# Splitting queries and keys for two attention heads at once, with a DMA that moves the second head's rows

## The chip, the core and the metric

The kernel runs on one core of one Trainium2 chip. A core has five engines with a queue of instructions each, all working in order within their own queue: PE (TensorE, matrix products into PSUM), DVE (VectorE), ACT (ScalarE), POOL (GpSimd) and SP (SyncE, which here only issues DMAs). An instruction that waits on a semaphore holds up everything behind it in its own queue. The metric is the device time of one execution in microseconds (us), as a median over runs.

## The reference

One layer of a hybrid block on 512 tokens of 1024 features in float32: a gated linear attention (GLA) branch and a latent attention (MLA) branch are gated, added, projected, and followed by a feed-forward network. The change lies in the MLA branch, which computes this:

```python
q = (rmsnorm(cq, g_q) @ w_uq).reshape(B, S, H, 96)          # 8 heads, 64 plain + 32 rotary features
q = concatenate([q[..., :64], rope(q[..., 64:], positions)]) * 96 ** -0.5
kv = (rmsnorm(ckv, g_kv) @ w_ukv).reshape(B, S, H, 64 + 128)
k_nope, v = kv[..., :64], kv[..., 64:]
k = concatenate([k_nope, broadcast(rope(kr, positions))])    # the 32 rotary features are the same for all heads
p = softmax(q @ k.T)                                         # per head, 512 x 512
o = p @ v
```

## The kernel before

Every float32 operand of a product is split into a high part (rounded to the PE's fp32r format, by an ACT copy) and a low part (what is left, by a DVE subtraction). A product is then three PE passes, hi·hi, hi·lo and lo·hi (`mm3`, lines 88 to 90). `split` (lines 93, 94) makes the two parts; `split_scaled` (lines 97, 98) does so with a factor.

The MLA branch works head by head, and its inputs are made for a pair of heads at a time by the generator `up_units(pr)`, for the pairs 0 to 3:

- It loads the pair's weights (`wq…f`, `wk…f`, lines 1011 and 1017) and splits them on ACT and POOL.
- For each of the two heads a tile `q{pr}{i}` of 128 partitions x 2 x 512 (high and low part beside each other) is taken. Its partitions 0 to 63 are to hold the plain features, partitions 64 to 95 the rotary ones. The rotary rows were computed for all heads before, in the tiles `ro`; a DMA per half of 16 rows brings them (line 1034), two per head.
- `uq{pr}` is the product that gives the plain features of both heads in one PSUM tile: head 2·pr in partitions 0 to 63, head 2·pr+1 in partitions 64 to 127. Two calls of `split_scaled`, on 64 partitions each, write the parts to partitions 0 to 63 of the two `q` tiles.
- `uk{pr}` is the same for the keys. The parts go to partitions 0 to 63 of two of the four lasting tiles `kbuf0` to `kbuf3` (pairs 0 and 2 use 0 and 1, pairs 1 and 3 use 2 and 3). Partitions 64 to 95 of each `kbuf` hold the rotary key rows, written once by `rotary_k_split` (line 891) and never again.
- `uv{pr}` gives the values, in two tiles `v`.

The attention loop runs over n, four steps per head (a step is 128 queries), in a software pipeline. At step n it issues the scores of the step (`att_scores`: the product `s`, its row maximum `top` on DVE, line 1071, the exponential `e` on ACT, line 1076), the normalisation of an earlier pair of steps (lines 1081 to 1083), the transposition of step n-3 (`att_flip`: four transposes `tp` on PE, line 1091, then a split into `pT`), and every second step the product with the values (`av`, 24 passes for a head in two halves). The units of `up_units` for the next pair are spread between these steps. From line 1300 on other work is laid in too: the loads and sums of the output projection's weights (`bo10f`, `bo11f`, `bo20f`, `bo21f`, `w`), on SP and POOL.

The order on the queues in the attention loop is chosen by a scheduler at build time, under a few ordering hints (`goes_behind`); from the output projection on, PE, ACT and DVE keep the order of the program text.

Names used below: `s`, `tp`, `av`, `uq`, `uk`, `uv` with a head or pair number, so s of head 2 is the first score product that needs `q10` (pair 1, first head) and `kbuf2`.

Of the kernel before, what the change touches and what calls it, by code (L numbers as in the profile page):

```python
# [27 lines left out]
HALF = ROPE // 2  # L28
QK_SCALE = float((NOPE + ROPE) ** -0.5)
# [27 lines left out]
def tile_block(ctx: ExitStack, tc: tile.TileContext, t, out: bass.AP):  # L57
    nc = tc.nc
# [5 lines left out]
    def tl(shape, dt, tag, bufs, name):  # L64
        serial[0] += 1
        return sb.tile(shape, dt, tag=tag, bufs=bufs, name=f"{name}_{serial[0]}")
# [4 lines left out]
    def u4(name, dt=F32R, shape=(P, 2, S)):  # L71
        return tl(list(shape), dt, "u4", 26, name)
# [4 lines left out]
    def ps(tag, name):  # L77
        serial[0] += 1
        return pp.tile([P, S], F32, tag=tag, bufs=4, name=f"{name}_{serial[0]}")
# [4 lines left out]
    def raw(x):  # L84
        return x.bitcast(F32)

    def mm3(acc, lh, ll, rh, rl, start, stop, onto=False):
        nc.tensor.matmul(acc, lh, rh, start=start, stop=False, skip_group_check=onto)  # L88
        nc.tensor.matmul(acc, lh, rl, start=False, stop=False, skip_group_check=onto)  # L89
        nc.tensor.matmul(acc, ll, rh, start=False, stop=stop, skip_group_check=onto)  # L90

    def split(hi, lo, src, rest=nc.vector):
        nc.scalar.activation(hi, src, AF.Copy)  # L93
        rest.tensor_tensor(lo, src, raw(hi), op=ALU.subtract)  # L94

    def split_scaled(hi, lo, src, scale):
        nc.scalar.activation(hi, src, AF.Copy, scale=scale)
        nc.vector.scalar_tensor_tensor(lo, src, scale, raw(hi), op0=ALU.mult, op1=ALU.subtract)
# [8 lines left out]
    def traced():  # L107
        return len(nc.cur_bb.bb.instructions)
# [102 lines left out]
    def stage(nk, nw, name):  # L211
        wf = tl([P, nk, nw], F32, "wf", 3, f"{name}f")
        return wf

    def halves(nk, nw, name):
        wh = tl([P, nk, nw], F32R, "wh", 4, f"{name}h")
        wl = tl([P, nk, nw], F32R, "wl", 4, f"{name}l")
        return wh, wl
# [599 lines left out]
    def up_T(wh, wl, src, name):  # L818
        acc = ps("mm", name)
        n = len(src)  # L820
        for k in range(n):
            mm3(acc, wh[:, k, :], wl[:, k, :], src[k][:, 0, :], src[k][:, 1, :], k == 0, k == n - 1)
        return acc
# [38 lines left out]
    def rotary_q(accs):  # L862
        res = []
        for x in range(2):
            a, b = u2(f"roa{x}"), u2(f"rob{x}")
            ta, tb = (cos, sin) if x == 0 else (sin, cos)
            nc.vector.scalar_tensor_tensor(a, accs[0], QK_SCALE, ta, op0=ALU.mult, op1=ALU.mult)
            nc.vector.scalar_tensor_tensor(b, accs[1], QK_SCALE, tb, op0=ALU.mult, op1=ALU.mult)
            nc.vector.tensor_tensor(a, a, b, op=ALU.subtract if x == 0 else ALU.add)
            hl = u4(f"ro{x}")  # L870
            split(hl[:, 0, :], hl[:, 1, :], a)
            res.append(hl)
        return res
# [9 lines left out]
    def rotary_k_split():  # L883
        r = slice(64, 96)
        res = []
        for b in range(4):
            kb = u4(f"kbuf{b}")
            if b == 0:
                split(kb[r, 0, :], kb[r, 1, :], kr[r])
            else:  # L890
                nc.sync.dma_start(raw(kb[r]), raw(res[0][r]))
            res.append(kb)
        return res
# [113 lines left out]
    def up_units(pr):  # L1007

        wq = stage(3, P, f"wq{pr}")
        for k in range(3):  # L1010
            nc.sync.dma_start(
                wq[:, k, :].rearrange("p (h e) -> p h e", h=2), w_uq[:, k, 2 * pr : 2 * pr + 2, 0:NOPE]
            )
        wqh, wql = halves(3, P, f"wq{pr}")
        split(wqh, wql, wq, nc.gpsimd)
        wk = stage(2, 384, f"wk{pr}")
        nc.sync.dma_start(
            wk.rearrange("p k (h e) -> p k h e", h=2), w_ukv[:, :, 2 * pr : 2 * pr + 2, :]
        )
        wh, wl = halves(2, 384, f"wk{pr}")  # L1020
        src = wk.rearrange("p k (h e) -> p k h e", h=2)
        for k in range(2):
            for c, e in ((slice(0, 128), slice(0, NOPE)), (slice(128, 384), slice(NOPE, 192))):
                split(wh[:, k, c].rearrange("p (h e) -> p h e", h=2),
                      wl[:, k, c].rearrange("p (h e) -> p h e", h=2), src[:, k, :, e], nc.gpsimd)
        if pr == 0:
            yield
        qs = []
        for i in range(2):
            q = u4(f"q{pr}{i}")  # L1030
            h = (2 * pr + i) * HALF
            for x in range(2):
                at = NOPE + x * HALF
                nc.sync.dma_start(raw(q[at : at + HALF]), raw(ro[x][h : h + HALF]))
            qs.append(q)
        yield
        accq = up_T(wqh, wql, cq, f"uq{pr}")
        for i in range(2):
            split_scaled(qs[i][0:64, 0, :], qs[i][0:64, 1, :], accq[i * 64 : i * 64 + 64, :], QK_SCALE)
        yield  # L1040
        acck = up_T(wh[:, :, 0:128], wl[:, :, 0:128], ckv, f"uk{pr}")
        for i in range(2):
            kb = kbuf[2 * (pr % 2) + i]
            split(kb[0:64, 0, :], kb[0:64, 1, :], acck[i * 64 : i * 64 + 64, :])
        yield
        vs = []
        for j in range(2):
            acc = ps("mm", f"uv{pr}{j}")
            for i in range(2):
                tok = slice((2 * j + i) * P, (2 * j + i + 1) * P)  # L1050
                for k in range(2):
                    mm3(acc[:, i * 256 : i * 256 + 256], ckv[k][:, 0, tok], ckv[k][:, 1, tok],
                        wh[:, k, 128:384], wl[:, k, 128:384], k == 0, k == 1)
            hl = u4(f"v{pr}{j}", F32R, (P, 2, 2, 256))
            flat = [hl[:, x].rearrange("p a b -> p (a b)") for x in range(2)]
            split_scaled(*flat, acc, 0.5)
            vs.append(hl)
            yield
        for i in range(2):
            heads[2 * pr + i] = (qs[i], kbuf[2 * (pr % 2) + i], vs, slice(i * MV, (i + 1) * MV))  # L1060
# [99 lines left out]
    for n, (a, m) in enumerate(steps[:-4]):  # L1160
# [4 lines left out]
        if steps[n + 1] in fillers:  # L1165
            at = traced()
# [106 lines left out]
    h = GH - 1  # L1273
# [10 lines left out]
    kbuf = rotary_k_split()  # L1284
# [5 lines left out]
    ckv = ckv_.normed()  # L1290
    accs = [up_T(*w, cq, f"ro{x}") for x, w in enumerate(wr)]
    units = up_units(0)
    next(units)
    ro = rotary_q(accs)
# [9 lines left out]
    at = traced()  # L1304
# [5 lines left out]
    in_program_order(pooled, (mybir.EngineType.Pool,))  # L1310
    LAG_B, LAG_C = 3, 6
    units = up_units(1)
    at = traced()
    next(units)
# [3 lines left out]
    for n in range(4 * MH + LAG_C - 1):  # L1318
# [12 lines left out]
        if 2 <= n % 8 < 7:  # L1331
            at = traced()
# [5 lines left out]
        if n in (6, 14):  # L1338
            units = up_units(n // 8 + 2)
            at = traced()  # L1340
            next(units)
            if n == 6:
                goes_behind((at, traced()), span["fourth"], SPLITTERS[:1])
# [28 lines left out]
        if n == 17:  # L1372
            at = traced()
# [246 lines left out]
    at = traced()  # L1620
# [9 lines left out]
    at = traced()  # L1630
# [7 lines left out]
    at = traced()  # L1638
# [12 lines left out]
    at = traced()  # L1651
# [81 lines left out]
```

## Time and profile before

| what | value |
|---|---|
| median of 3 runs | 757.4 us (757.4 to 757.45) |
| the profiled execution, its own time | 757.7 us |
| its span, first to last instruction | 755.7 us |
| instructions | 10257 |
| HBM read, written | 83.25 MB, 2.10 MB |
| first score product to the last of the attention loop's steps | about 298 to 376 us of the span |

Times within an execution are counted from the start of the span. A line of a profile names the engine, the source line and operation, the tile written and the tiles read, the shapes, how often it occurs, and after a bar the busy time and the mean duration of one in ns. PEld is the PE's loading of weights, SPq the issuing of a DMA by SP. "To landing" is the time from a DMA's issue until its completion arrives.

### The profile page before, as it was taken

To read this page: it belongs to the slowest core of one execution; us is meant where nothing else is said; L and a number is where in the kernel's file an instruction comes from. 1 tells how busy PE (TensorE), PEld (TensorE's weight loads), DVE (VectorE), ACT (ScalarE), POOL (GpSimd) and SP (SyncE) were. 2 spreads that over 40 slices of the span, in tenths; PEclk is the share of its full clock that TensorE was granted. 3 is DMA by queue.
4 is the path that set the end of the run, shared out by engine and by line. 5 is a ranking of instruction groups with operands and counts; after the bars stand their busy time and mean duration, and the time that the engine had idled before them with its cause. 6 is when DMAs were issued, how large, how long until landed. Compare 5 with 4: busy or idle time off the path is not lost.

```text
span 755.7 us, 10257 instructions
## 1 busy us (share of the span) xinstructions
PE 746.8 (99%) x3720; PEld 632.8 (84%) x3720; DVE 586.5 (78%) x850; ACT 461.6 (61%) x780; POOL 165.3 (22%) x238
## 2 busy tenths in 40 slices
PE   9999999999999999999999999999999999999996
PEld 7888888888889888898888988888888888888885
DVE  7777887989787597898897787856696578748795
ACT  8456565686476575988865766345544555345644
POOL 0722110262662632136850100000000000000014
PEclk9999999999999999999999999999999999999999
DMA  9849582611321334228897421461126410650003
GB/s 315 256 125 230 177 174 82 113 29 29 83 57 31 47 86 114 73 84 198 264 201 227 129 57 56 140 194 57 56 65 204 122 57 4 206 153 0 29 1 111
DMA packets 94306, 87.59 MB, mean 116 GB/s; under 512 B 15696, under 2 KB 66896, under 8 KB 94256
## 3 DMA queue, kind: packets, MB, share of 16 engines
q1 hardware_dynamic: 87760, 74.33, 32.8%
q0 software_dynamic: 6208, 12.32, 9.3%
q8 instruction: 29, 0.48, 0.3%
q10 hardware_dynamic: 288, 0.28, 0.1%
q14 instruction: 21, 0.17, 0.1%
HBM read 83.25 MB, written 2.10 MB: 113 GB/s over the span
## 4 chain that ended last, share of the span: by engine, by line
PE 93%; DVE 3%; ACT 2%; DMA 1%; issue 1%; POOL 0%; POOLq 0%; ACTq 0%; SPq 0%
PE f L90 8%; PE f L88 8%; PE f L89 8%; PE gx L88 4%; PE gx L90 4%; PE gx L89 4%; PE first L330 3%; PE gz L90 2%; PE gz L88 2%; PE gz L89 2%; PE zb L88 1%; PE tp L1091 1%; PE zb L90 1%; PE zb L89 1%; PE wox L88 1%; PE wox L90 1%
## 5 line engine op out<-in xcount | busy, mean ns | idle before, releaser
L1672 POOL DMA_DIRECT2D gfin<-in_g_final x1 | 0.6, 628 | 284.1 <-PE f L90 284.1
L961 DVE TENSOR_TENSOR w<-w,w 128x1024 f32<-128x1024 f32 x32 | 38.7, 1221 | 0.3
L1071 DVE TENSOR_REDUCE top<-s 128x1 f32<-128x512 f32 x32 | 21.8, 682 | 2.9 <-PE s L90 2.6
L1076 ACT ACTIVATE e<-s,top 128x512 f32<-128x512 f32 x32 | 22.0, 689 | 2.7 <-DVE top L1071 2.4
L94 DVE TENSOR_TENSOR pT<-tp,pT 128x512 fp32r<-128x512 f32 x32 | 21.6, 682 | 2.4 <-ACT pT L93 2.2
L1399 DVE TENSOR_TENSOR h<-h,gx 128x512 f32<-128x512 f32 x32 | 21.5, 682 | 1.9 <-PE gx L90 1.8
L93 ACT ACTIVATE pT<-tp 128x512 fp32r<-128x512 f32 x32 | 18.9, 597 | 3.2 <-PE tp L1091 3.0
L1091 PE MATMUL tp<-ident,e 128*128 128x128 f32 x128 | 19.3, 274 | 0.4 <-ACT e L1082 0.2
L88 PE MATMUL av<-pT,v 128*128 128x256 f32 x64 | 18.9, 296 | 0.0
L93 ACT ACTIVATE ghb<-y 128x512 fp32r<-128x512 f32 x16 | 10.1, 633 | 14.0 <-DVE y L907 14.0
L1465 ACT ACTIVATE fa<-f 128x512 f32<-128x512 f32 x32 | 18.5, 578 | 0.0
L1091 PEld LDWEIGHTS tp<-ident,e 128*128 128x128 f32 x128 | 15.1, 140 | 3.9 <-ACT e L1082 0.8
L89 PE MATMUL av<-pT,v 128*128 128x256 f32 x64 | 18.2, 285 | 0.0
L90 PE MATMUL av<-pT,v 128*128 128x256 f32 x64 | 18.2, 285 | 0.0
L547 ACT ACTIVATE bds<-bd 128x512 f32<-128x512 f32 x4 | 2.4, 598 | 20.9 <-PE bd L543 20.9
L93 ACT ACTIVATE b_00h<-w 128x1024 fp32r<-128x1024 f32 x7 | 7.4, 1061 | 12.6 <-PE gz L90 6.0
L93 ACT ACTIVATE b_20h<-w 128x1024 fp32r<-128x1024 f32 x7 | 7.4, 1062 | 12.1 <-PE gz L90 6.0
L93 ACT ACTIVATE b_10h<-w 128x1024 fp32r<-128x1024 f32 x7 | 7.4, 1061 | 12.1 <-PE gz L90 6.0
L88 PE MATMUL s<-kbuf,q 96*128 96x512 f32 x32 | 14.2, 444 | 0.1
L1474 ACT ACTIVATE px<-fa 128x256 f32<-128x256 f32 x32 | 13.4, 418 | 1.0
L957 POOL DMA_DIRECT2D w<-in_w_out x10 | 12.3, 1401 | 6.5 <-DVE bo60l L94 5.3
L636 POOL DMA_DIRECT2D gvw<-in_w_in x4 | 4.8, 1226 | 38.7 <-DVE gvw L641 34.0
(1731 smaller groups left out, 2947.8 us busy)
## 6 DMA issues: line engine op xcount, KB each, us to landing
w<-in_w_ff SPq DMA_DIRECT2D x64, 256.0 KB, 3.4
w<-in_w_out POOLq DMA_DIRECT2D x10, 512.0 KB, 8.8
grw<-in_w_in SPq DMA_DIRECT2D x8, 512.0 KB, 9.3
zaw<-in_w_in SPq DMA_DIRECT2D x8, 512.0 KB, 7.9
gvw<-in_w_in SPq DMA_DIRECT2D x8, 512.0 KB, 4.5
w<-in_w_out SPq DMA_DIRECT2D x16, 256.0 KB, 5.9
x<-in_xt SPq DMA_DIRECT2D x8, 256.0 KB, 5.2
vw<-in_w_first SPq DMA_DIRECT2D x8, 256.0 KB, 5.4
```

Source lines behind the costliest of these rows:

```text
L88: nc.tensor.matmul(acc, lh, rh, start=start, stop=False, skip_group_check=onto)
L89: nc.tensor.matmul(acc, lh, rl, start=False, stop=False, skip_group_check=onto)
L90: nc.tensor.matmul(acc, ll, rh, start=False, stop=stop, skip_group_check=onto)
L93: nc.scalar.activation(hi, src, AF.Copy)
L94: rest.tensor_tensor(lo, src, raw(hi), op=ALU.subtract)
L330: nc.tensor.matmul(f_accs[i], a[:, i * P : (i + 1) * P], b, start=k == 0 and x == 0, stop=k == KD - 1 and x == 2)
L961: nc.vector.tensor_tensor(wq[dst][g], wq[x][g], wq[y][g], op=op)
L1071: nc.vector.tensor_reduce(top, acc, axis=AX.X, op=ALU.max, negate=True)
L1076: nc.scalar.activation(e, acc, AF.Exp, bias=top, accum_out=tot[:, qt % 2 : qt % 2 + 1])
L1091: nc.tensor.transpose(tp[:, k * P : (k + 1) * P], e[:, k * P : (k + 1) * P], ident)
L1399: nc.vector.tensor_tensor(hc, hc, acc, op=op)
L1465: nc.scalar.activation(a, acc, AF.Relu)
```

## The change

Pair 0 stays as it was (`apart`). For pairs 1 to 3:

- The split of `uq` is one `split_scaled` over all 128 partitions into the first head's tile. A DMA moves partitions 64 to 127 of it to partitions 0 to 63 of the second head's tile. After it two DMAs bring the first head's rotary rows to its partitions 64 to 95, which the split and the move had used. The second head's rotary rows still come before the product, as they did.
- The split of `uk` is one `split` over all 128 partitions into the first of the pair's two `kbuf` tiles. It overwrites the rotary key rows there. A DMA moves partitions 64 to 127 to the second `kbuf`, and another brings the rotary rows (partitions 64 to 95) back from the second `kbuf` to the first.

```diff
@@ -1025,23 +1025,38 @@
-        qs = []
-        for i in range(2):
-            q = u4(f"q{pr}{i}")
+        def rotary_rows(i):
             h = (2 * pr + i) * HALF
             for x in range(2):
                 at = NOPE + x * HALF
-                nc.sync.dma_start(raw(q[at : at + HALF]), raw(ro[x][h : h + HALF]))
-            qs.append(q)
+                nc.sync.dma_start(raw(qs[i][at : at + HALF]), raw(ro[x][h : h + HALF]))
+        apart = pr == 0
+        qs = [u4(f"q{pr}{i}") for i in range(2)]
+        for i in range(2):
+            if apart or i == 1:
+                rotary_rows(i)
         yield
         accq = up_T(wqh, wql, cq, f"uq{pr}")
-        for i in range(2):
-            split_scaled(qs[i][0:64, 0, :], qs[i][0:64, 1, :], accq[i * 64 : i * 64 + 64, :], QK_SCALE)
+        if apart:
+            for i in range(2):
+                split_scaled(qs[i][0:64, 0, :], qs[i][0:64, 1, :], accq[i * 64 : i * 64 + 64, :], QK_SCALE)
+        else:
+            split_scaled(qs[0][:, 0, :], qs[0][:, 1, :], accq, QK_SCALE)
+            nc.sync.dma_start(raw(qs[1][0:64]), raw(qs[0][64:128]))
+            rotary_rows(0)
         yield
         acck = up_T(wh[:, :, 0:128], wl[:, :, 0:128], ckv, f"uk{pr}")
-        for i in range(2):
-            kb = kbuf[2 * (pr % 2) + i]
-            split(kb[0:64, 0, :], kb[0:64, 1, :], acck[i * 64 : i * 64 + 64, :])
+        kbs = kbuf[2 * (pr % 2) : 2 * (pr % 2) + 2]
+        if apart:
+            for i, kb in enumerate(kbs):
+                split(kb[0:64, 0, :], kb[0:64, 1, :], acck[i * 64 : i * 64 + 64, :])
+        else:
+            split(kbs[0][:, 0, :], kbs[0][:, 1, :], acck)
+            nc.sync.dma_start(raw(kbs[1][0:64]), raw(kbs[0][64:128]))
+            nc.sync.dma_start(raw(kbs[0][64:96]), raw(kbs[1][64:96]))
         yield
```

## The prediction

> **What bounds the kernel now.** First the page's busy shares and its chain of work that ended last.
>
> ```profile
> PE 746.8 (99%) x3720; PEld 632.8 (84%) x3720; DVE 586.5 (78%) x850; ACT 461.6 (61%) x780; POOL 165.3 (22%) x238
> PE 93%; DVE 3%; ACT 2%; DMA 1%; issue 1%; POOL 0%; POOLq 0%; ACTq 0%; SPq 0%
> ```
>
> PE is busy 99% of the span and is 93% of the chain. The averages hide the stages, so next the stretches: busy time of each engine in the attention loop and around it, then one crowded part of the loop, then PE's waits in the loop.
>
> ```profile
> core 0: us, PE busy (x) PEld busy (x) DVE busy (x) ACT busy (x) POOL busy (x), PEclk, DMA share, GB/s
> 284.00:298.00 14.00, 13.74 (x72) 11.72 (x71) 9.59 (x16) 6.99 (x14) 3.09 (x6) 1.00 0.43 87
> 298.00:382.00 84.00, 83.49 (x556) 74.64 (x555) 74.25 (x130) 73.71 (x159) 42.32 (x50) 1.00 0.56 152
> 382.00:420.00 38.00, 38.00 (x182) 31.80 (x182) 33.25 (x53) 23.36 (x44) 8.66 (x12) 1.00 0.88 228
> ...
> 310.00:320.00 10.00, 9.85 (x64) 8.64 (x63) 9.27 (x17) 10.00 (x24) 3.27 (x5) 1.00 0.45 110
> ...
> PE tp L1091 <- ACT e L1082: 0.2, 1, 0.2
> ```
>
> In the 84.00 us of the loop PE is busy 83.49: it stands still 0.51 us in all, and one named wait is 0.2 of it. DVE (74.25) and ACT (73.71) are nearly as full, and ACT has no idle time between 310 and 320, yet PE loses only 0.15 there. So PE's own work sets this stage's length, with the others close behind. The clock is at 1.00 throughout.
>
> **What is removed.** Per pair 1 to 3 the change takes away one ACT copy and one DVE operation for the queries, and as much for the keys. These groups give durations; the `v` rows are the same operations on 128 partitions.
>
> ```profile
> L97 ACT ACTIVATE v<-uv 128x512 fp32r<-128x512 f32 x6 | 3.6, 598 | 1.4 <-PE uv L90 1.2
> L97 ACT ACTIVATE q<-uq 64x512 fp32r<-64x512 f32 x6 | 3.6, 593 | 0.7 <-PE uq L90 0.4 <-DVE q L98 0.3
> L93 ACT ACTIVATE kbuf<-uk 64x512 fp32r<-64x512 f32 x6 | 3.6, 592 | 0.6 <-PE uk L90 0.5
> ...
> L94 DVE TENSOR_TENSOR kbuf<-uk,kbuf 64x512 fp32r<-64x512 f32 x6 | 4.1, 687 | 1.1 <-ACT kbuf L93 1.0
> L98 DVE SCALAR_TENSOR_TENSOR q<-uq,q 64x512 fp32r<-64x512 f32 x6 | 4.1, 687 | 0.9 <-ACT q L97 0.7
> L98 DVE SCALAR_TENSOR_TENSOR v<-uv,v 128x512 fp32r<-128x512 f32 x6 | 4.1, 683 | 0.0
> ```
>
> Doubling the partitions is free: 598 against 593 ns on ACT, 683 against 687 on DVE. So six instructions of 0.59 us leave ACT (3.6 us) and six of 0.69 leave DVE (4.1 us). Neither engine ends the stage. PE's instructions stay the same in number and shape, so what can come back is PE's idle time: at most 0.51 us, at least nothing. I take half, 0.3 us, because the named wait is on ACT and relief there should remove it, while other gaps follow from the scheduler's order and may reappear.
>
> **What is added.** Nine DMAs: for each pair a 256 KB move of `q` and one of `kbuf` (64 partitions of 4 KB), and a 128 KB return of the rotary key rows. Two rotary-row DMAs of the first head move from before `uq` to behind the move. None is on PE's path until a score product of the pair's first head waits for it. That product needs both ends of two chains: split, move, then rotary rows; split, move, then return. The second DMA of a chain overwrites rows that the first one reads, so SP must wait for the first landing. Before, the first head needed only its split. The second head, four steps later, needs only the moves. The landings of the trace, and what SP's issue takes:
>
> ```profile
> q<-ro SPq DMA_DIRECT2D x16, 64.0 KB, 2.3
> w<-in_w_out SPq DMA_DIRECT2D x16, 256.0 KB, 5.9
> bo11f<-in_w_out SPq DMA_DIRECT2D x2, 256.0 KB, 3.0
> ...
> kbuf<-kbuf SPq DMA_DIRECT2D x3, 128.0 KB, 3.6
> ...
> 290.65 2.42 SPq L1034 DMA_DIRECT2D q<-ro  x4
> ...
> 302.00:310.00 8.00, 8.00 (x56) 7.21 (x54) 5.36 (x10) 7.23 (x14) 0.00 (x0) 1.00 0.00 1
> 346.00:360.00 14.00, 13.77 (x100) 12.36 (x99) 12.73 (x22) 11.33 (x25) 8.73 (x10) 1.00 0.83 192
> ```
>
> No row shows a 256 KB move within SBUF. Below lies the 256 KB load at 3.0; above, the straight line through the two SBUF copies, 2.3 at 64 KB and 3.6 at 128 KB, gives 6.2. I take 3.6: the 128 KB copies shared the engines with weight loads, while the moves of pair 1 start in a stretch where the DMA engines do nothing (share 0.00). The return is the same operation as the copy at 3.6; bounds are 2.3 and 5.9 (the loads in the crowded stretch). An issue is 2.42/4 = 0.6 us.
>
> Pair 1, where the first head comes soonest. In time order: the splits, then the place of head 2 on PE.
>
> ```profile
> 304.51 0.67 DVE L98 SCALAR_TENSOR_TENSOR q<-uq,q 64x512 fp32r<-64x512 f32 x1
> 306.16 0.69 DVE L98 SCALAR_TENSOR_TENSOR q<-uq,q 64x512 fp32r<-64x512 f32 x1
> 306.89 0.69 DVE L94 TENSOR_TENSOR kbuf<-uk,kbuf 64x512 fp32r<-64x512 f32 x1
> ...
> 311.38 0.27 PE L1091 MATMUL tp<-ident,e 128*128 128x128 f32 x1
> ...
> 315.37 0.40 PE L88 MATMUL s<-kbuf,q 96*128 96x512 f32 x1
> ...
> 318.30 1.12 ACT L93 ACTIVATE bo11h<-bo11f 128x1024 fp32r<-128x1024 f32 x1
> ```
>
> `q10` is whole at 304.51 + 0.67 = 305.2. The key split moves up into the slot of the second query split, 306.16 to 306.9. Query chain: 305.2 + 3.6 = 308.8, two issues to 310.0; the second starts at 309.4 and lands 2.3 later, at 311.7. Key chain: 306.9 + 3.6 = 310.5, + 3.6 = 314.1. The build keeps head 2 at nearly the same place on PE: between the last transposes of head 0 (311.38) and s of head 2 it puts s of head 1, twenty `av` passes and one group of transposes, 0.35 + 0.7 + 20 x 0.12 + 0.35 = 3.8 us, so about 315.2. The margin is 315.2 - 314.1 = 1.1 us, by the lower bounds 306.9 + 3.0 + 2.3 = 312.2 it is 3.0, by the upper ones of an idle DMA (6.2 + 3.6) the data are 1.5 late.
>
> Behind these waits on SP stand the next pair's second-head rotary rows and `bo11f`: return issued at 310.5, three issues, `bo11f` at 312.3, landed 315.3, three us before ACT's split at 318.30. That is hidden by `bo11h`'s place late in ACT's queue.
>
> Pairs 2 and 3, by the first key split and the first score product of heads 4 and 6:
>
> ```profile
> 325.44 0.67 DVE L94 TENSOR_TENSOR kbuf<-uk,kbuf 64x512 fp32r<-64x512 f32 x1
> 346.36 0.68 DVE L94 TENSOR_TENSOR kbuf<-uk,kbuf 64x512 fp32r<-64x512 f32 x1
> ...
> 336.16 0.39 PE L88 MATMUL s<-kbuf,q 96*128 96x512 f32 x1
> 358.57 0.48 PE L88 MATMUL s<-kbuf,q 96*128 96x512 f32 x1
> ```
>
> In the build the scheduler has set the pair 2 split behind more DVE work, which I count as 0.7 later: 326.8 + 7.2 = 334.0 against 336.2, margin 2.2. Pair 3: 347.0 + 7.2 = 354.2 against 358.6, margin 4.4; with 5.9 for both, 358.8, just late, because DMA is 0.83 busy from 346 on. The loads `w` queued behind the pair 3 return start near 351; before, eight of them started at 352.
>
> ```profile
> 352.08 4.97 SPq L951 DMA_DIRECT2D w<-in_w_out  x8
> ```
>
> So nothing downstream moves either. The sum: 757.7 for the profiled execution - 0.3 + 0 for the DMAs = 757.4. That execution lies 0.3 above the median of 757.4, so the forecast for the median is 757.1, rounded to 757.2 for the chance of a small new gap.
>
> **The rivals.** *A, slower: the key rows of the pair's first head land late.* It decides once move plus return take longer than 315.2 - 306.9 = 8.3 us at head 2, or 336.2 - 326.8 = 9.4 at head 4. With 6.2 + 3.6 = 9.8 PE stands 1.5 us at head 2 and 0.4 at head 4: 757.2 + 1.9 = 759.1. With 6.2 + 5.9 it stands 3.8, 2.7 and 0.5: 764.2. For it speaks that no row shows such a move, and that PE has nothing else it may run, being in order; against it the 3.0 of `bo11f` and the empty DMA at 302 to 310. I price it at 760. The Trainium skill ("TensorE: Matmul & The Clock Gate", Part 1: the HAM clock gate) says that about 3.4 us of idling halves PE's clock until some 3.4 us of work have passed. By that page the worst case would cost about 1.7 us more (an estimate from its figures); no stretch quoted here idles long enough to show it.
>
> *B, slower: the new order of the queues makes waits of its own.* ACT and DVE are reordered through the loop. A PE wait in the loop is 0.2 us in the row above; one more for each of some twelve reordered steps would be 2.4 us: 759.6. Against it: ACT and DVE have less to do than before.
>
> *C, faster: ACT and DVE bound the loop, and PE's busy time covers waits.* For it: ACT's 10.00 of 10.00. Then ACT's 3.6 us come off: 753.8. Against it: start to start, score passes run at the pace of passes where nothing else is crowded.
>
> ```profile
> 295.29 0.39 PE L88 MATMUL zb<-xT,zb7h 128*128 128x512 f32 x1
> 295.52 0.39 PE L89 MATMUL zb<-xT,zb7h 128*128 128x512 f32 x1
> ...
> 298.01 0.40 PE L88 MATMUL s<-kbuf,q 96*128 96x512 f32 x1
> 298.25 0.40 PE L89 MATMUL s<-kbuf,q 96*128 96x512 f32 x1
> ```
>
> Both steps are 0.23 to 0.24 us. The Trainium skill ("Perfetto Trace Analysis", Identifying the Most-Contended Engine) holds that matmul busy share is a poor measure of how near PE is to its limit, since matmuls are pipelined, and that the weight-load share should be used. By that share the loop has 74.64 of 84 us, so the page leaves room for C; the pace just shown speaks against it.
>
> That the change does nothing it says is excluded: the build has six ACT and six DVE instructions fewer and nine DMAs more.
>
> **How the numbers follow.** About 0.2%, 1.5 us, is what a measurement of this kernel can tell from no change. Forecast (757.2, own range 756.4 to 758.6): 0.66. A: 0.20, of which a quarter stays under 1.5 us. B: 0.08, half of it under. C: 0.06, all over. So faster 0.06, slower 0.15 + 0.04 = 0.19, raised to 0.22 because A's prices rest on an operation that no row shows; same 0.72. The range reaches to A's priced case with some room above and stops short of C: 756.3 to 760.3.
>
> **What would show it.** Right: `q` and `kbuf` groups with three 128x512 entries each; the moves landing in 3 to 4 us; s of heads 2, 4 and 6 without idle time before them; PE idle in the loop at or below 0.5 us; a span within 1 us of 755.7. Wrong: idle time of PE ahead of s of head 2, released by a DMA (A); PE waits on ACT or DVE scattered through the loop (B); a loop shorter by more than 1 us at full PE (C).

## The result and the profile after

The changed kernel takes 762.2 us (median of 6 runs, 761.6 to 762.9); the kernel before takes 757.5 us on the same chip (median of 6, 757.4 to 758.3). The ratio is 1.0061, 95% interval 1.0050 to 1.0072. The change makes the kernel slower by 4.7 us, where no measurable change was forecast (757.2, range 756.3 to 760.3).

Shares of the span first (engine, busy us, share, instructions), then the groups of ACT for the two splits inside the attention loop. Both are of the changed kernel.

```profile
PE 748.7 (99%) x3720; PEld 634.6 (83%) x3720; DVE 582.5 (77%) x844; ACT 457.6 (60%) x774; POOL 164.2 (22%) x238
```

```profile
L97 ACT ACTIVATE q<-uq 128x512 fp32r<-128x512 f32 x3 | 1.8, 595 | 0.0
L93 ACT ACTIVATE kbuf<-uk 128x512 fp32r<-128x512 f32 x3 | 1.8, 591 | 1.4 <-PE uk L90 1.4
```

The change did what it says: six instructions fewer on ACT (780 to 774) and on DVE (850 to 844), and one on 128 partitions costs what one on 64 did (595 and 591 against 593 and 592 ns). ACT and DVE are 4.0 us less busy each. And PE, whose instructions are the same, is 1.9 us *more* busy (746.8 to 748.7). A busy time that grows with the same work is a sign to look at the clock. First the waits of PE, then stretches of the loop: length, busy time of PE, PEld, DVE, ACT and POOL, granted clock, DMA share, GB/s.

```profile
PE s L88 <- DMA kbuf<-kbuf: 3.0, 1, 3.0
```

```profile
298.00:382.00 84.00, 81.00 (x534) 72.65 (x533) 65.79 (x118) 65.82 (x146) 39.37 (x48) 0.98 0.68 175
358.00:360.00 2.00, 0.00 (x0) 0.00 (x0) 1.14 (x3) 0.45 (x1) 2.00 (x4) 1.00 1.02 228
...
362.00:363.00 1.00, 1.00 (x4) 0.70 (x4) 0.62 (x2) 0.86 (x2) 0.00 (x0) 0.57 0.94 315
363.00:364.00 1.00, 1.00 (x6) 0.94 (x5) 1.00 (x2) 0.41 (x2) 0.00 (x0) 0.50 0.85 283
364.00:365.00 1.00, 1.00 (x7) 1.00 (x7) 0.06 (x1) 0.84 (x3) 0.00 (x0) 0.50 1.11 256
365.00:366.00 1.00, 1.00 (x8) 1.00 (x8) 0.00 (x0) 0.42 (x1) 0.00 (x0) 0.73 1.05 242
```

There is one stop of PE, 3.0 us, and it is the whole idle time of the loop (84.00 - 81.00). Behind it the granted clock falls to 0.57, 0.50, 0.50 and 0.73 in four successive microseconds: 0.43 + 0.50 + 0.50 + 0.27 = 1.7 us of PE time lost while PE counts as busy. Stop and clock make 4.7 us of PE time. That the medians differ by 4.7 us too is in part chance, since the change also gains about 1 us; the account stands further down. The chain of waits shows where the stop stands (start, us, what).

```profile
352.17 0.34 SPq L1032
...
352.56 0.60 SPq L1032
...
353.27 7.32 DMA kbuf<-kbuf
...
360.73 0.47 PE s L88
```

The first score product of head 6 waits for the return of the rotary key rows of pair 3, issued at 353.27 and landed at 360.59. Next SP's queue, then the DMAs issued in that stretch with KB and us from issue to landing.

```profile
342.05 0.42 SPq L967 DMA_DIRECT2D bo21f<-in_w_out  x1
342.57 0.38 SPq L224 DMA_DIRECT2D f00f<-in_w_ff  x1
344.48 0.50 SPq L1048 DMA_DIRECT2D q<-q  x1
346.99 0.50 SPq L1058 DMA_DIRECT2D kbuf<-kbuf  x1
351.96 1.19 SPq L1032 DMA_DIRECT2D q<-ro  x2
353.27 0.53 SPq L1059 DMA_DIRECT2D kbuf<-kbuf  x1
```

```profile
w<-in_w_out POOLq DMA_DIRECT2D x2, 512.0 KB, 8.3
f00f<-in_w_ff SPq DMA_DIRECT2D x1, 512.0 KB, 8.0
...
q<-q SPq DMA_DIRECT2D x1, 256.0 KB, 7.4
kbuf<-kbuf SPq DMA_DIRECT2D x1, 256.0 KB, 5.7
q<-ro SPq DMA_DIRECT2D x2, 64.0 KB, 7.0
kbuf<-kbuf SPq DMA_DIRECT2D x1, 128.0 KB, 7.3
```

The query move needs 7.4 us and lands at 351.9. SP waits for it before it may issue the rotary rows, and the return stands behind these two issues although the key move landed at 346.99 + 5.7 = 352.7, which costs it 0.6 us. Then the return itself takes 7.3 us, beside two accumulating loads of `w` from POOL's queue. Pair 1, in an empty stretch, is the contrast:

```profile
q<-q SPq DMA_DIRECT2D x1, 256.0 KB, 2.9
kbuf<-kbuf SPq DMA_DIRECT2D x1, 256.0 KB, 2.8
...
kbuf<-kbuf SPq DMA_DIRECT2D x1, 128.0 KB, 2.3
```

The same three kinds of copy take 2.3 to 2.9 us there, and heads 2 and 4 start without a wait. So the trace leaves a theory and rivals: are pair 3's copies slow because of what stands ahead of them in SP's queue (`f00f`), because of the bytes of `f00f` and of POOL's loads whatever their queue, or because three copies in a chain are too many in any case?

### The profile page after: what moved, and what is told of

It is laid out like the page before. It is cut to its first block, busy times and chain, and to the rows that moved or that the text cites. A ratio compares the mean times of both kernels' runs of the same rounds, so it can differ in the third digit from the quotient of the medians.

```text
span 760.1 us, 10265 instructions
## 1 busy us (share of the span) xinstructions
PE 748.7 (99%) x3720; PEld 634.6 (83%) x3720; DVE 582.5 (77%) x844; ACT 457.6 (60%) x774; POOL 164.2 (22%) x238
## 4 chain that ended last, share of the span: by engine, by line
PE 95%; DVE 2%; DMA 1%; ACT 1%; issue 0%; POOL 0%; SPq 0%; POOLq 0%
PE f L88 8%; PE f L90 8%; PE f L89 8%; PE gx L88 4%; PE gx L90 4%; PE gx L89 4%; PE first L330 3%; PE gz L88 2%; PE gz L90 2%; PE gz L89 2%; PE tp L1106 2%; PE zb L88 1%; PE zb L90 1%; PE zb L89 1%; PE s L88 1%; DMA kbuf<-kbuf 1%
## 5 line engine op out<-in xcount | busy, mean ns | idle before, releaser
L1097 ACT ACTIVATE e<-e,tot 128x512 f32<-128x512 f32 x16 | 11.6, 725 | 4.5 <-DVE tot L1096 4.5
```

## The experiments

Each kernel was run beside the kernel before on one chip. The medians of before in these comparisons are 757.8 to 757.9 us.

**Pair 3 left apart.**

```diff
-        apart = pr == 0
+        apart = pr in (0, 3)
```

> The last pair (heads 6 and 7) is split head by head again; pairs 1 and 2 keep the common split and the moves. Theory 1 (the loss is the last pair's chain of copies: its first score product waits 3.0 us for the returned key rows, because the copies meet weight loads, and the clock drops behind the stop): no PE wait before heads 2, 4 and 6, granted clock 1.00 through the loop, time within 1 us of before, 756.7 to 758.0. Rival 2 (common splits cost something in every pair, by order or by DMA): about two thirds of the loss stays, 760.5. Rival 3 (the loss comes from nine more DMAs on SP that hold up the weight loads): six of the nine stay, 760.5, with the loads late.

Measured: 756.7 us (756.4 to 757.2, 10 runs), ratio 0.9985, interval 0.9975 to 0.9994. The loop, in the same columns as above:

```profile
298.00:382.00 84.00, 83.97 (x561) 75.44 (x560) 71.52 (x127) 71.43 (x155) 42.82 (x51) 1.00 0.65 171
```

PE stands still 0.03 us and the clock is 1.00. All of the loss belongs to pair 3; two pairs with copies are slightly faster than none.

**Pair 3 alone.**

```diff
-        apart = pr == 0
+        apart = pr != 3
```

> Only the last pair has the common split and the moves; pairs 1 and 2 are split head by head. Theory 1: the whole loss stays, 761 to 763, with a PE wait of 2 to 4 us before head 6 and a halved clock behind it. Rivals 2 and 3: a third of the loss, about 759.

Measured: 757.4 us (756.3 to 762.8, 10 runs), ratio 1.0006, interval 0.9986 to 1.0027. That is a miss as a median. The runs fall into two groups: seven lie between 756.3 and 757.9 with a mean granted clock of 0.998 or 0.999 over the span, three at 761.1, 761.2 and 762.8 with 0.994 to 0.996. The scheduler had put the query move ahead of `f00f` here, which the edit did not ask for. SP's queue and the landings of the profiled execution, one of the short ones:

```profile
344.48 0.52 SPq L1048 DMA_DIRECT2D q<-q  x1
345.09 0.53 SPq L224 DMA_DIRECT2D f00f<-in_w_ff  x1
```

```profile
q<-q SPq DMA_DIRECT2D x1, 256.0 KB, 3.8
```

Issued 0.6 us ahead of the 512 KB, the move takes 3.8 us instead of 7.4. The return is issued at 351.33 and takes 5.6 us, so it lands at 356.9, only 0.3 us ahead of head 6's first score product (357.23). The three long runs, with their lower clock, would fit a margin that is sometimes missed and then costs a stop and a drop of the clock together; no trace of them was taken, so this is not shown.

**Queries only**: the keys are split head by head, as before.

```diff
-        if apart:
+        if True:
             for i, kb in enumerate(kbs):
```

> Only the queries of pairs 1 to 3 have the common split and move; the keys are split head by head, so no key rows are moved or returned. Theory 1, with the query chain alone: the last pair's rotary rows, issued only when the move has landed, were down at 358.7 and 359.8 beside the return; without the key copies they land about 1 us sooner, 358.5 to 359, so PE still waits 1 to 1.5 us before head 6: 759.0 to 760.5. If only the return of the key rows is at fault: no wait, 757 to 758.

Measured: 759.3 us (758.7 to 761.7, 9 runs), ratio 1.0028, interval 1.0018 to 1.0039. PE's wait, and the stretches of that execution:

```profile
PE s L88 <- DMA q<-ro: 1.8, 1, 1.8
```

```profile
359.00:360.00 1.00, 0.72 (x3) 0.63 (x4) 0.81 (x3) 0.12 (x1) 1.00 (x3) 1.00 0.53 195
360.00:361.00 1.00, 1.00 (x8) 0.85 (x7) 1.00 (x2) 0.91 (x2) 1.00 (x2) 1.00 0.95 256
```

Without any key copy head 6 still waits, for its rotary query rows. The query chain is a second, nearly as late one, as the changed kernel's own trace says: there the first head's two rotary rows land at 358.7 and 359.8, and PE was ready at 357.7. The 1.8 us is not a clean price of that chain, since in this build four more 256 KB loads of `w` stand ahead of the query move on SP and the move is issued 1.2 us later (345.70). After this 1.8 us stop the clock stays at 1.00.

**Keys only**: the queries are split head by head, and both heads' rotary rows come before `uq`.

```diff
-            if apart or i == 1:
-                rotary_rows(i)
+            rotary_rows(i)
...
-        if apart:
+        if True:
             for i in range(2):
                 split_scaled(
```

> Only the keys of pairs 1 to 3 have the common split, move and return; the queries are split head by head. Theory 1: the return no longer stands behind the rotary rows on SP and is issued when the move lands, about 352.5, but meets the same accumulating loads and takes 6 to 7 us: 358.5 to 359.5, PE waits 1 to 2 us, 759.5 to 761. If the query chain that held SP (4.4 us wait for the move's landing) is what makes the return late: no wait, 757 to 758.

Measured: 758.2 us (757.2 to 759.2, 10 runs), ratio 1.0003, interval 0.9994 to 1.0013. The wait came, but elsewhere. PE's wait, and SP's queue in the stretch of pair 1:

```profile
PE s L88 <- DMA kbuf<-kbuf: 1.2, 1, 1.2
```

```profile
311.19 0.80 SPq L967 DMA_DIRECT2D bo11f<-in_w_out  x2
312.08 0.52 SPq L1058 DMA_DIRECT2D kbuf<-kbuf  x1
```

The expected place, head 6, was wrong: there the key chain alone is on time. The wait is at head 2, where in this build two 256 KB loads stand ahead of pair 1's return and the return takes 4.6 us instead of 2.3. That looks like the same fault in another pair, and suggests that the full change's good pairs are good by the scheduler's order; no run tested it.

**The loads out of the way.** `f00f` is wanted late: in the changed kernel its split starts at 415.7 us, 65 us after it landed.

```profile
L93 ACT ACTIVATE f00h<-f00f x1: 1062/1062/1062, 415.7 to 415.7; 128x1024 fp32r<-128x1024 f32 x1
```

Three kernels keep the whole change and move loads only. The first puts `f00f` behind both moves on SP's queue (n = 19 is the loop step that issues the key move):

```diff
             next(units, None)
+            if n == 19:
+                span["moved"] = at, traced()
...
     early = [proj_begin(w1, 0, "f00", "mm")]
-    goes_behind((at, traced()), span["sums"], SP_ONLY)
+    goes_behind((at, traced()), span["moved"], SP_ONLY)
```

> The whole change, but the 512 KB load of f00f is ordered behind the two moves of the last pair on SyncE's queue instead of ahead of them; all else as in the changed kernel. Theory 1 (the last pair's moves stand behind 512 KB on the same ring and their rows come 3 us too late for head 6): the query move of pair 3 lands 3 to 4.5 us after its issue instead of 7.4, the two loads of rotary rows and the return of the last 32 rows follow some 3 us sooner, the return lands at 355.5 to 357.5 and head 6's first score product goes on time near 357.5. Wait of TensorE on kbuf under 0.3 us, granted clock 1.00 there, 755.9 to 757.3 us; single executions may still be near 761 if the margin is thin. Theory 2 (the ring's order is not it; POOL's accumulating loads from 349.8 us on slow whatever is under way): the query move is faster but the return still takes 6 to 7 us and lands after 358.5, wait 1 to 2.5 us, 758 to 761 us.

Measured: 756.8 us (756.3 to 758.4, 11 runs), ratio 0.9990, interval 0.9981 to 0.9999; three of the runs lie at 758.0 to 758.4, of which no trace was taken. Landings in the stretch of pair 3:

```profile
q<-q SPq DMA_DIRECT2D x1, 256.0 KB, 5.0
...
kbuf<-kbuf SPq DMA_DIRECT2D x1, 128.0 KB, 5.7
```

The return, issued at 349.96, lands at 355.7, 1.0 us ahead of head 6 (356.70).

The second leaves `f00f` ahead of the moves and issues POOL's accumulating loads later:

```diff
-        if n == 20:
+        if n == 25:
             load_onto(B11, B12, w_out)
...
-        if n == 23:
+        if n == 26:
             load_onto(B21, B11, w_out)
```

> The whole change, but POOL's four accumulating loads of the output weights (2 at 349.8 and 350.7 us, 2 at 359.4 and 360.1 us in the changed kernel) are issued behind the merged sums of pair 1, several us later; f00f stays ahead of the moves on SyncE's queue. Theory 1: the query move still takes near 7.4 us, so the rotary rows are still issued near 352, but with the engines freer they and the return land in 3 to 5 us: head 6 starts 0 to 1.5 us late, without a clock step, 756.5 to 758.5 us. Theory 2 (POOL's loads alone): the return lands in 2.3 to 4 us, no wait, 756 to 757 us; if POOL's loads do nothing, wait 3 us and 761 to 763 us as with the change.

Measured: 757.2 us (756.4 to 757.4, 11 runs), ratio 0.9988, interval 0.9979 to 0.9997.

```profile
q<-q SPq DMA_DIRECT2D x1, 256.0 KB, 7.5
kbuf<-kbuf SPq DMA_DIRECT2D x1, 256.0 KB, 5.6
...
kbuf<-kbuf SPq DMA_DIRECT2D x1, 128.0 KB, 2.4
```

The two edits answer to two halves of the delay, which the landings of these traces keep apart. Behind `f00f` the moves take 7.5 and 5.6 us, whatever POOL does. Beside POOL's loads the return takes 5.7 us (first kernel) and 7.3 (the change), and without them 2.4. With either half removed head 6 starts in time: in the changed kernel it takes both to make the stop.

The third kernel has both edits.

> Both edits at once: f00f behind the last pair's moves on SyncE's queue and POOL's accumulating loads later. Both theories: the moves land in 3 to 4.5 us, the return in 2.3 to 4 us near 353 to 355, no wait of TensorE in the attention loop, granted clock 1.00, 755.8 to 757 us in every execution, without the jumps to 761. If POOL's later loads make their readers in the output stage late instead, a wait on w2 appears after 382 us and the time is 1 to 4 us more.

Measured: 756.8 us (756.2 to 757.3, 11 runs), ratio 0.9985, interval 0.9976 to 0.9994. Landings, and the loop:

```profile
q<-q SPq DMA_DIRECT2D x1, 256.0 KB, 3.7
...
kbuf<-kbuf SPq DMA_DIRECT2D x1, 128.0 KB, 2.3
```

```profile
298.00:382.00 84.00, 84.00 (x561) 75.39 (x560) 71.38 (x125) 70.49 (x153) 42.69 (x50) 1.00 0.70 180
```

Here pair 3's chain is nearly as fast as pair 1's, the return is at 2.3 us although `f00f` now follows right behind it, as in the first of the three, and PE loses nothing. The query moves of the first kernel and of this one, 5.0 and 3.7 us behind the same loads on SP, differ for a reason that was not found. This kernel beats the changed one and, by about 1 us, the one before; so does the first experiment.

**Queue or bytes?** The last kernel issues `f00f` from ScalarE, on its own queue, right behind the activation that makes the queries of pair 3 (n = 18 is the step of the query split).

```diff
             next(units, None)
+            if n == 18:
+                span["unit"] = at, traced()
...
+        if n == 23:
+            at = traced()
+            span["f00"] = stage(KD, P, "f00")
+            nc.scalar.dma_start(span["f00"], w1[:, 0:P].rearrange("(k p) w -> p k w", p=P))
+            goes_behind((at, traced()), span["unit"], SPLITTERS[:1])
...
-    early = [proj_begin(w1, 0, "f00", "mm")]
-    goes_behind((at, traced()), span["sums"], SP_ONLY)
+    wf = span["f00"]
+    wh, wl = halves(KD, P, "f00")
+    split(wh, wl, wf)
+    early = [(wh, wl, ps("mm", "f00"))]
```

> The whole change, but the 512 KB load of f00f is issued by ScalarE, on its own DMA queue, right behind the activation that writes the queries of the last pair (near 344 us, as the query move), instead of by SyncE at 342.6; the same bytes are under way at the same time, on another queue. Theory 1a (order on SyncE's queue: the query move is served after the 512 KB ahead of it): the query move lands 3 to 4.5 us after its issue, before f00f, the rotary rows and the return land by 357.5, wait under 0.5 us, 756 to 757.5 us. Theory 1b (the 16 DMA engines are full, whichever queue the bytes stand in): the query move and f00f share the engines and the move still takes 6 to 8 us, the rotary rows are issued at 351 to 352 and the return lands at 359 to 361 behind POOL's loads, wait 1.5 to 3 us, 758 to 762 us. ScalarE gives some 0.5 us for the issue; should this make the probabilities late for TensorE, a wait on ACT of about as much appears near 345.

Measured: 762.0 us (759.2 to 763.0, 6 runs), ratio 1.0043, interval 1.0028 to 1.0058. PE's wait, then the issue by ACT, the issue of the query move by SP, and the move's landing:

```profile
PE s L88 <- DMA kbuf<-kbuf: 3.3, 1, 3.3
```

```profile
343.18 0.39 ACTq L1390 DMA_DIRECT2D f00f<-in_w_ff  x1
```

```profile
344.08 0.50 SPq L1048 DMA_DIRECT2D q<-q  x1
```

```profile
q<-q SPq DMA_DIRECT2D x1, 256.0 KB, 7.1
```

The order on SP's queue falls as the cause, and the bytes stand. With no `f00f` in SP's queue at all, but the same 512 KB issued 0.9 us ahead of the move (343.18 against 344.08), the move takes 7.1 us and the stop is there again. The DMA engines are full in both: in the rows from 344 to 350 their busy share is 1.06, 0.96 and 0.99 in the changed kernel, 1.01, 1.19 and 0.88 here. The Trainium skill ("DMA: Bandwidth & Descriptors", Issuing engines are not separate DMA queues) says that DMAs from whichever engine end on the same 16 DMA engines and mix there; this trace agrees, 7.1 us from a separate queue against 7.4 us in one queue.

## Why the prediction was wrong

**What was right.** The 128-partition operations cost the same. Moves and return in an empty stretch were taken at 3.6 us; they took 2.9, 2.8 and 2.3. Heads 2 and 4, which I held to be the dangerous ones, had no wait. Rival A is what happened, with its mechanism (the key rows of a pair's first head land late, PE in order behind them) and not with its place: I set its deciding points at heads 2 and 4.

**The step that failed** is pair 3: "347.0 + 7.2 = 354.2 against 358.6, margin 4.4". Three things in it were wrong.

- *The size of the landings.* The return landed at 360.6, not 354.2. Of these 6.4 us the key move has 2.1 (5.7 instead of 3.6), the return 3.7 (7.3 instead of 3.6), and 0.6 passed on SP between the key move's landing and the return's issue. I had quoted the row that warned of it, 0.83 busy DMA engines from 346 to 360, and used it only for an upper case ("with 5.9 for both, 358.8, just late"). In a stretch that is 0.83 busy on average the upper case was the likely one, and the return's 7.3 us went beyond even its 5.9. What is under way in that stretch could be read from the trace of before: 512 KB of `f00f` and POOL's loads.

```profile
343.48 0.38 SPq L224 DMA_DIRECT2D f00f<-in_w_ff  x1
...
349.73 2.51 POOL L957 DMA_DIRECT2D w<-in_w_out  x2
```

- *The reference point.* The row at 358.57 is head 6's second step. The first starts 1.05 us sooner, which takes the upper case from "just late" to 1.3 us late. The row that should have been taken, from the timeline of before:

```profile
357.52 0.40 PE L88 MATMUL s<-kbuf,q 96*128 96x512 f32 x1
```

- *The query chain was left out for pair 3.* Both chains were worked out for pair 1 only. In pair 3 the query move holds SP until 351.9, and the return queues behind its rows. The rows themselves land at 359.8, 2.1 us after PE was ready, and the kernel without any key copy stopped too.

**The price.** I gave A 760 us. The stop measures 3.0 us, inside the 1.5 to 3.8 that I worked out for head 2 alone; that it fits is luck, since it stands at another head and comes from other terms. What was missing is the 1.7 us of slow clock, which I had mentioned beside the price and not counted in it. The Trainium skill ("TensorE: Matmul & The Clock Gate", Part 1: the HAM clock gate) speaks of some 3.4 us idle and half the clock, which makes a penalty of 1.7 us by my estimate from its figures. The trace agrees in the clock (0.50) and in the 1.7 us, but shows them after a stop of 3.0 us, shorter than the 3.4.

**The gain was under-sized.** I bounded it by PE's idle time, 0.51 us, and took 0.3. The first and the last start of the 32 score steps give the loop's length; of before, of the change, and of the change with both loads moved:

```profile
L88 PE MATMUL s<-kbuf,q x32: 389/474/499, 298.0 to 370.4; 96*128 96x512 f32 x32
```

```profile
L88 PE MATMUL s<-kbuf,q x32: 389/474/547, 298.6 to 374.8; 96*128 96x512 f32 x32
```

```profile
L88 PE MATMUL s<-kbuf,q x32: 389/474/500, 298.2 to 369.5; 96*128 96x512 f32 x32
```

72.4, 76.2 and 71.3 us. With the copies on time the loop is 1.1 us shorter; the medians differ by 1.0 (757.8 to 756.8). So rival C had a grain of truth: PE's busy time covers some 0.6 us that its idle time of 0.51 does not show. Where the 0.6 comes from was not traced. The gain does not grow in proportion to the instructions removed: the same rows give 71.4 us with pairs 1 and 2 alone and 71.7 with pair 3 alone, so a part may lie in the scheduler's order.

The change's loop is 4.9 us longer than the same change's with both loads moved, of which the stop and the clock explain 3.0 + 1.7 = 4.7. Against before, the loop is 3.8 us longer and the span 4.4. The other 0.6 lies ahead of the first score product (298.6 against 298.0), whose start varies between 297.8 and 298.8 among the kernels here; it is not shown to be a price of the change. Behind the loop nothing differs (385.3 us from the last of these starts to the end in both). So the gain of 1.1 was there, and a DMA that came 3 us late gave it back more than four times over.

Rival B did not show in the changed kernel: its only wait of PE in the loop is that DMA.

## What to carry to other kernels

A copy that is put on a dependent chain must be costed in the stretch where it runs, with the bytes that are already under way there, for each place where it occurs and not for the first only. Before adding one, look for bulk loads issued just ahead of it and ask when their data are wanted: here a load wanted 65 us later, together with POOL's loads, decided the sign, and moving it behind the copies, at no cost that the runs show, turned a loss of 0.6% into a small gain. Issuing that load from another engine's queue did not help here, while the 16 DMA engines were full.

## What was not expected of the hardware

A short stop of PE has a second price, and that one jumps. The execution with a 1.8 us stop kept its clock at 1.00; after 3.0 us the changed kernel lost 1.7 us, and the last kernel, after 3.3 us, ran at half its clock for longer. The stretches of the last:

```profile
361.00:362.00 1.00, 1.00 (x4) 0.60 (x4) 0.00 (x0) 0.00 (x0) 0.39 (x1) 0.50 0.73 176
...
366.00:367.00 1.00, 1.00 (x7) 1.00 (x6) 0.00 (x0) 0.40 (x1) 0.00 (x0) 0.50 1.09 238
```

The clock is at 0.50 from 361 until 367, which costs 3.0 us. With the stop of 3.3 that makes 6.3 of the 6.5 us by which its loop (77.8 us) is longer than the 71.3. Whether the clock drops seems to differ from run to run of one kernel. Of the last kernel's runs two lie at 759.2 and 759.5 with a mean clock of 0.998, four between 761.8 and 763.0 with 0.994 to 0.996; with the queries only, five lie at 758.7 to 759.3 with 0.998, four at 760.9 to 761.7 with 0.996 or 0.997. The mean clocks fit a drop of the clock in the upper group, but do not prove it: 0.997 also stands with short runs, such as the traced one of the kernel with both loads moved, whose clock is 1.00 throughout the loop. Of each kernel only one run was traced. How a 256 KB copy issued 0.9 us behind 512 KB takes twice as long as one issued 0.6 us ahead of it (7.1 and 3.8 us), on another queue too, was measured but its mechanism inside the DMA engines stays open.
